# A log-sum-exp over rows of 1024: eighteen loads with another taper, a first load of two rows, and the second load ahead of the opening barrier

## The chip, the cores and the metric

The kernel runs on one core of one Trainium2 chip. The metric is the device time of one execution in microseconds (us), median of several. The *span* is shorter: it goes from the first to the last instruction of the program in the trace. Each timed run lists both. Two more words: the *opening barrier* is the point near the start of the program where the engines wait for each other, and the *taper* is the run of ever smaller loads at the end. Engines are named ScalarE (ACT), VectorE (DVE), GpSimd (POOL) and SyncE (SP); SyncE issues the loads.

## The reference

```python
x = np.random.randn(32, 512, 1024).astype(np.float32)      # 67 MB
x_max = np.max(x, axis=-1, keepdims=True)
out = x_max.squeeze(-1) + np.log(np.sum(np.exp(x - x_max), axis=-1))
```

16384 rows of 1024 are spread over 128 partitions, so each partition has 128 rows of 4 KB. The kernel leaves the maximum out, which the values allow, and computes log(sum(exp(x))).

## The kernel before

A list says how many rows each load takes, how many of them VectorE sums (ScalarE sums the rest with its accumulator), in how many pieces ScalarE takes VectorE's rows, and whether VectorE adds the two halves of each row in one pass:

```python
CHUNKS = [   # rows, rows summed by VectorE, pieces, by halves
    (4, 4, 1, False), (15, 15, 1, False), (16, 16, 2, False), (16, 16, 2, False),
    (16, 15, 2, False), (14, 14, 2, False), (13, 12, 2, False), (9, 8, 1, False),
    (7, 7, 1, True), (5, 4, 1, True), (4, 3, 1, True), (3, 3, 1, False), (2, 2, 1, True),
    (1, 0, 1, False), (1, 0, 1, False), (1, 0, 1, False), (1, 0, 1, False),
]
RING_ROWS = 51          # the loads land in a ring of 51 rows per partition
```

```python
    def load(i):        # waits until the engines have left these rows of the ring
        ...
        nc.sync.dma_start(out=ring[:, s : s + r], in_=x_v[:, row : row + r]).then_inc(landed[i], 16)
    ...
    load(0)
    n_early = len(body.instructions)        # what is there so far goes ahead of the opening barrier
    ...
    for i, (r, n_dve, parts, by_halves) in enumerate(CHUNKS):
        if i:
            load(i)
        ...
        if i == len(CHUNKS) - 1:            # logarithm of all but the last four rows
            take_logs(logged, late_row, sums[:, logged:late_row], *done_before[-LATE])
        nc.scalar.wait_ge(landed[i], 16)
        for lo, hi in cuts(n_dve, parts):
            nc.scalar.activation(out=ring[:, s+lo : s+hi], in_=ring[:, s+lo : s+hi], func=Exp).then_inc(act_done, 1)
            ...                             # VectorE sums these rows, row by row by halves or all at once
        for j in range(n_dve, r):
            nc.scalar.activation(..., func=Exp, accum_out=total(row + j)).then_inc(act_done, 1)
    take_logs(late_row, NB, late[:, : NB - late_row], dves, acts)
    nc.scalar.dma_start(out=out_v, in_=res).then_inc(stored, 16)
```

The sizes shrink so that the last load is a single row.

The softmax here doesn't subtract the row's maximum and nothing guards it: scores larger than these inputs give would overflow.

Of the kernel before, what the change touches and what calls it, by code (L numbers as in the profile page):

```python
# [8 lines left out]


CHUNKS = [
    (4, 4, 1, False), (15, 15, 1, False), (16, 16, 2, False), (16, 16, 2, False),
    (16, 15, 2, False), (14, 14, 2, False), (13, 12, 2, False), (9, 8, 1, False),
    (7, 7, 1, True), (5, 4, 1, True), (4, 3, 1, True), (3, 3, 1, False), (2, 2, 1, True),
    (1, 0, 1, False), (1, 0, 1, False), (1, 0, 1, False), (1, 0, 1, False),
]
RING_ROWS = 51

# [8 lines left out]
def kernel(  # L27
# [57 lines left out]
    def cuts(n, parts):  # L85
        ends = [-(-n * k // parts) for k in range(parts + 1)]
        return [(lo, hi) for lo, hi in zip(ends, ends[1:]) if lo < hi]

    def load(i):
        (s, row), r = place[i], CHUNKS[i][0]  # L90
        act_wait = max(a for a, _ in busy[s : s + r])
        dve_wait = max(d for _, d in busy[s : s + r])
        if dve_wait:
            nc.sync.wait_ge(dve_done, dve_wait)
        if act_wait:
            nc.sync.wait_ge(act_done, act_wait)
        nc.sync.dma_start(out=ring[:, s : s + r], in_=x_v[:, row : row + r]).then_inc(
            landed[i], 16
        )

    def take_logs(lo, hi, src, dve_wait, act_wait):
        nonlocal acts
        nc.scalar.wait_ge(act_done, act_wait)
        nc.scalar.wait_ge(dve_done, dve_wait)
        nc.scalar.activation(out=res[:, lo:hi], in_=src, func=Ln).then_inc(act_done, 1)  # L105
        acts += 1
# [4 lines left out]
    def total(t):  # L111
        return late[:, t - late_row : t - late_row + 1] if t >= late_row else sums[:, t : t + 1]

    body = nc.main_func.blocks[-1]
    assert not body.instructions
    load(0)
    n_early = len(body.instructions)

    nc.scalar.preload_act_table_set("natural_log_exp_and_others")  # L119
# [1 line left out]
    logged = 0  # L121
    done_before = [(0, 0)]
    for i, (r, n_dve, parts, by_halves) in enumerate(CHUNKS):
        if i:
            load(i)
        s, row = place[i]
        if i == LN_AT:
            logged = place[i - LN_LAG][1]
            take_logs(0, logged, sums[:, :logged], *done_before[i - LN_LAG])
        if i == len(CHUNKS) - 1:  # L130
# [3 lines that stand above are left out]
            nc.scalar.activation(  # L134
                out=ring[:, s + lo : s + hi], in_=ring[:, s + lo : s + hi], func=Exp
            ).then_inc(act_done, 1)
            acts += 1
            nc.vector.wait_ge(act_done, acts)
            if by_halves:
                for j in range(lo, hi):  # L140
                    nc.vector.tensor_tensor_reduce(  # L141
                        out=ring[:, s + j, : D // 2],
                        in0=ring[:, s + j, : D // 2],
                        in1=ring[:, s + j, D // 2 :],
                        scale=1.0,
                        scalar=0.0,
                        op0=Add,
                        op1=Add,
                        accum_out=sums[:, row + j : row + j + 1],
                    ).then_inc(dve_done, 1)  # L150
                    dves += 1
                    busy[s + j] = (0, dves)
            else:
                nc.vector.reduce_sum(  # L154
                    out=sums[:, row + lo : row + hi], in_=ring[:, s + lo : s + hi], axis=AX
                ).then_inc(dve_done, 1)
                dves += 1
                for j in range(lo, hi):
                    busy[s + j] = (0, dves)
        for j in range(n_dve, r):  # L160
            nc.scalar.activation(  # L161
                out=ring[:, s + j],
                in_=ring[:, s + j],
                func=Exp,
                accum_out=total(row + j),
            ).then_inc(act_done, 1)
            acts += 1
            busy[s + j] = (acts, 0)
        done_before.append((dves, acts))
# [64 lines left out]
```

## Time and profile before

| | before |
|---|---|
| time, median of 3 runs | 163.15 us |
| span of the profiled run | 161.4 us |
| input queue busy | 96.9% of the span |
| ScalarE, VectorE busy | 71%, 75% |
| last exponential starts | 158.46 us |

The lines that carry this stand in the prediction. One more belongs here, the end of VectorE's timeline (start, duration, instruction): the last step of its last sum, by halves of one row.

```profile
158.14 0.08 DVE L141 DVE_READ_ACCUMULATOR2_ANT sums<- 128x1 f32 x1
```

It ends at 158.22, and ScalarE's logarithm of these sums starts at 158.32. The last row is in at 158.4: its load was issued at 130.2 and took 28.2.

### The profile page before, as it was taken

To read this page: it belongs to the slowest core of one execution; us is meant where nothing else is said; L and a number is where in the kernel's file an instruction comes from. 1 tells how busy PE (TensorE), PEld (TensorE's weight loads), DVE (VectorE), ACT (ScalarE), POOL (GpSimd) and SP (SyncE) were. 2 spreads that over 40 slices of the span, in tenths; PEclk is the share of its full clock that TensorE was granted. 3 is DMA by queue.
4 is the path that set the end of the run, shared out by engine and by line. 5 is a ranking of instruction groups with operands and counts; after the bars stand their busy time and mean duration, and the time that the engine had idled before them with its cause. 6 is when DMAs were issued, how large, how long until landed. Compare 5 with 4: busy or idle time off the path is not lost.

```text
span 161.4 us, 149 instructions
## 1 busy us (share of the span) xinstructions
DVE 121.0 (75%) x46; ACT 115.1 (71%) x40; POOL 0.2 (0%) x4
## 2 busy tenths in 40 slices
DVE  0028000003999999999999699999999999999892
ACT  3170005996079960999519993999199999999995
POOL 0000000000000000000000000000000000000000
DMA  6999699989989989989979999999999999999990
GB/s 256 508 487 457 289 472 520 406 374 520 422 357 520 406 374 520 406 374 520 406 341 455 455 455 439 422 422 422 430 429 429 418 426 415 427 430 417 403 394 24
DMA packets 2592, 67.18 MB, mean 416 GB/s; under 512 B 288, under 2 KB 416, under 8 KB 928
## 3 DMA queue, kind: packets, MB, share of 16 engines
q1 hardware_dynamic: 2448, 67.11, 96.9%
q10 hardware_dynamic: 144, 0.07, 0.1%
HBM read 67.11 MB, written 0.07 MB: 416 GB/s over the span
## 4 chain that ended last, share of the span: by engine, by line
DMA 49%; DVE 29%; ACT 20%; issue 0%
DMA ring<-in_x_dram 49%; DVE sums L154 29%; ACT ring L134 17%; ACT ring L161 3%; ACT res L105 0%
## 5 line engine op out<-in xcount | busy, mean ns | idle before, releaser
L154 DVE TENSOR_REDUCE sums<-ring 128x8 f32<-128x8192 f32 (+5 forms) x14 | 111.2, 7995 | 37.3 <-ACT ring L134 37.2
L134 ACT ACTIVATE ring<-ring 128x8192 f32<-128x8192 f32 (+6 forms) x18 | 104.4, 5835 | 43.9 <-DMA ring<-in_x_dram 43.8
L141 DVE CUSTOM_DVE_ANT_0 ring<-ring 128x512 f32<-128x512 f32 x16 | 9.9, 688 | 0.0
L161 ACT ACTIVATE ring<-ring 128x1024 f32<-128x1024 f32 x9 | 9.3, 1041 | 0.0
L119 ACT ACT_TABLE_LOAD x1 | 1.3, 1283 | 0.8 <-PEq L215 0.8
L161 ACT ACTIVATION_READ_ACCUMULATOR ring<-ring 128x1 f32 x9 | 1.5, 172 | 0.0
L141 DVE DVE_READ_ACCUMULATOR2_ANT sums<- 128x1 f32 x16 | 1.3, 84 | 0.0
L105 ACT ACTIVATE res<-sums 128x81 f32<-128x81 f32 (+1 forms) x2 | 0.5, 246 | 0.0
L105 ACT ACTIVATE res<-late 128x4 f32<-128x4 f32 x1 | 0.2, 173 | 0.0
L215 POOL MEMSET const-bfloat16-1.0<- 128x1 bf16 x1 | 0.1, 103 | 0.0
L215 POOL MEMSET const-uint8-127<- 128x1 uint8 x1 | 0.1, 102 | 0.0
L215 POOL MEMSET const-float32-0.0<- 128x1 f32 x1 | 0.1, 100 | 0.2 <-issue 0.2
L215 POOL MEMSET const-float32-1.0<- 128x1 f32 x1 | 0.1, 99 | 0.0
## 6 DMA issues: line engine op xcount, KB each, us to landing
ring<-in_x_dram SPq DMA_DIRECT2D x1, 7680.0 KB, 25.2
ring<-in_x_dram SPq DMA_DIRECT2D x1, 7168.0 KB, 28.6
ring<-in_x_dram SPq DMA_DIRECT2D x1, 6656.0 KB, 35.7
ring<-in_x_dram SPq DMA_DIRECT2D x1, 4608.0 KB, 20.2
ring<-in_x_dram SPq DMA_DIRECT2D x2, 2048.0 KB, 16.1
ring<-in_x_dram SPq DMA_DIRECT2D x1, 3584.0 KB, 28.3
ring<-in_x_dram SPq DMA_DIRECT2D x1, 2560.0 KB, 27.3
ring<-in_x_dram SPq DMA_DIRECT2D x4, 512.0 KB, 27.0
```

What stands on the lines that cost most here:

```text
L105: nc.scalar.activation(out=res[:, lo:hi], in_=src, func=Ln).then_inc(act_done, 1)
L119: nc.scalar.preload_act_table_set("natural_log_exp_and_others")
L134: nc.scalar.activation(out=ring[:, s + lo : s + hi], in_=ring[:, s + lo : s + hi], func=Exp).then_inc(act_done, 1)
L141: nc.vector.tensor_tensor_reduce(out=ring[:, s + j, : D // 2], in0=ring[:, s + j, : D // 2], in1=ring[:, s + j, D // 2 :], scale=1.0, scal ...
L154: nc.vector.reduce_sum(out=sums[:, row + lo : row + hi], in_=ring[:, s + lo : s + hi], axis=AX).then_inc(dve_done, 1)
L161: nc.scalar.activation(out=ring[:, s + j], in_=ring[:, s + j], func=Exp, accum_out=total(row + j),).then_inc(act_done, 1)
L215: nc = _bacc.Bacc("TRN2", target_bir_lowering=False, num_devices=1)
```

## The change

The intent: data reach the engines earlier (two rows first, the second load issued before the barrier), and less work is left when the last row lands (a finer taper).

```diff
 CHUNKS = [
-    (4, 4, 1, False), (15, 15, 1, False), (16, 16, 2, False), (16, 16, 2, False),
-    (16, 15, 2, False), (14, 14, 2, False), (13, 12, 2, False), (9, 8, 1, False),
-    (7, 7, 1, True), (5, 4, 1, True), (4, 3, 1, True), (3, 3, 1, False), (2, 2, 1, True),
-    (1, 0, 1, False), (1, 0, 1, False), (1, 0, 1, False), (1, 0, 1, False),
+    (2, 2, 1, False), (14, 14, 1, False), (14, 14, 1, False), (13, 13, 2, False),
+    (15, 15, 2, False), (14, 13, 2, False), (13, 13, 2, False), (12, 9, 2, False),
+    (7, 7, 2, False), (7, 7, 1, True), (5, 4, 1, False), (3, 3, 2, True), (3, 3, 1, True),
+    (2, 2, 1, True), (1, 0, 1, False), (1, 0, 1, False), (1, 0, 1, False), (1, 0, 1, False),
 ]
@@
     load(0)
+    load(1)
     n_early = len(body.instructions)
@@
-        if i:
+        if i > 1:
             load(i)
```

## The prediction

In its lines of ScalarE's timeline, brackets hold the idle time before an instruction and what ended it. In its table of half microseconds the columns are the stretch, its length, the busy time (and count) of VectorE, ScalarE and GpSimd, TensorE's clock (not used here), the DMA engines' share and GB/s.

The 433 GB/s is what the queue moved. The sum comes to 0.07 us of queue and 0.06 of rounding and ScalarE lateness, 0.13 together, and 163.15 + 0.13 - 0.1 gives the centre of 163.2. The 0.1 for the start is my estimate of how much of the measured 0.67 and 0.34 could be cured. The 0.15 of start in VectorE's 14 x 1.067 + 0.15 follows from the rows by form: 3 rows take 3.353, and 3.353 - 3 x 1.067 = 0.15. The "nearer 1 us" to the first byte is this kernel's: issue at 0.00, nothing moved before 1.00.

> **What bounds the kernel now.** I read the page first: what is busy, then which chain ended last. All 128 rows of 4 KB per partition come in through one queue, and that queue is busy nearly all the time.
>
> ```profile
> span 161.4 us, 149 instructions
> DVE 121.0 (75%) x46; ACT 115.1 (71%) x40; POOL 0.2 (0%) x4
> ...
> q1 hardware_dynamic: 2448, 67.11, 96.9%
> ```
>
> The reader should see that VectorE and ScalarE have a quarter of the span to spare, while the input queue fills 96.9% of it. So the middle is a matter of bytes, and only the two ends can be shortened. ScalarE's timeline gives the landings of the large loads, because in the middle it waits for each:
>
> ```profile
> 7.49 3.62 ACT L134 ACTIVATE ring<-ring 128x4096 f32<-128x4096 f32 x1 [5.43 <-DMA ring<-in_x_dram]
> 25.99 13.00 ACT L134 ACTIVATE ring<-ring 128x15360 f32<-128x15360 f32 x1 [14.89 <-DMA ring<-in_x_dram]
> 45.36 13.95 ACT L134 ACTIVATE ring<-ring 128x8192 f32<-128x8192 f32 x2 [6.36 <-DMA ring<-in_x_dram]
> ...
> 84.08 13.10 ACT L134 ACTIVATE ring<-ring 128x8192 f32<-128x8192 f32 x2 [5.39 <-DMA ring<-in_x_dram]
> ...
> 116.74 10.54 ACT L134 ACTIVATE ring<-ring 128x6144 f32<-128x6144 f32 x2 [3.49 <-DMA ring<-in_x_dram]
> ```
>
> From 45.36 to 84.08 two loads of 16 rows land: 19.36 us each. Last I read the end of the chain of waits:
>
> ```profile
> 122.44 24.70 DMA ring<-in_x_dram
> 147.14 0.02 issue
> 147.16 2.76 ACT ring L134
> 149.92 1.04 ACT ring L161 x2
> 150.96 4.45 ACT ring L134 x2
> 155.42 3.01 ACT ring L161 x6
> 158.43 0.01 ACT res L105
> 158.43 0.03 issue
> 158.46 1.11 ACT ring L161 x2
> ```
>
> From 116.74 (row 94) to 147.16 (row 119) 25 rows come in four loads, 30.42 us. At the big loads' rate, 25/16 x 19.36 = 30.25; the 0.17 too much is the price of 4 - 25/16 = 2.44 loads more, so one load costs 0.07 us and one row (19.36 - 0.07)/16 = 1.206 us. After 147.16 ScalarE waits for nothing and ends the kernel. It is hardly later than the data: the first load landed at 7.49, so its queue began, in effect, at 7.49 - 4 x 1.206 - 0.07 = 2.60; the second took 18.50 instead of 15 x 1.206 + 0.07 = 18.16, another 0.34; the last row is then due at 2.94 + 128 x 1.206 + 17 x 0.07 = 158.50, and ScalarE's last exponential began at 158.46. The model misses by 0.04 at most. So **transfer and ScalarE end together**. From 158.46 to the end (161.41) is 2.95 us of exponential, logarithm and store, which the change leaves alone.
>
> [...] 16 rows are 8.39 MB, in 19.36 us 433 GB/s. [...] Here the first issue is at 0.00 and the trace by half microseconds shows nothing before 1.00, so nearer 1 us, then a ramp:
>
> ```profile
> 0.50:1.00 0.50, 0.00 (x0) 0.23 (x1) 0.00 (x0) 1.00 0.00 0
> 1.00:1.50 0.50, 0.00 (x0) 0.50 (x1) 0.00 (x0) 1.00 1.11 229
> 1.50:2.00 0.50, 0.00 (x0) 0.50 (x1) 0.00 (x0) 1.00 0.68 197
> 2.00:2.50 0.50, 0.00 (x0) 0.06 (x1) 0.00 (x0) 1.00 0.69 295
> 2.50:4.50 2.00, 0.00 (x0) 0.00 (x0) 0.00 (x0) 1.00 1.03 442
> ```
>
> [...]
>
> **The change part by part.** ScalarE's price, from the rows by form: 13.002 us for 15 rows and 1.893 for 2 give 0.854 us a row and 0.18 an instruction. Back to back half of the 0.18 overlaps (two of 7.02 take 13.95), so an instruction costs 0.09 on the path. A row summed on ScalarE costs 1.04, in the last four loads 1.00 (they start at 155.32, 156.32, 157.32). VectorE: (16.154 - 3.353)/12 = 1.067 a row.
>
> *One load more.* 17 become 18 over the same 128 rows: +0.07 us of queue. The last row is due at 158.57.
>
> *Second load ahead of the barrier.* Its issue moves from 0.78 us to some 0.4. But it queues behind the first, which holds the queue until 7.49 now and until 2.60 + 2 x 1.206 + 0.07 = 5.1 with two rows. An issue at 0.78, with 1 us to its first byte, was there in time and still would be. Worth 0. The barrier and the table load behind it (1.28 us, from 0.77) come about 0.4 us later and end near 2.5, before the 5.1 at which ScalarE has data: 0.
>
> *First load of two rows.* ScalarE and VectorE begin 2.4 us earlier on two rows, then wait for the second load (16 rows, due 22.4). They have slack there: 0 for the end.
>
> *Middle sizes and the ring of 51 rows.* The first four loads now fill 43 rows and the fifth (15) wraps to slot 0, so it waits for VectorE on the second load: due 22.4, exponential 14 x 0.854 + 0.18 = 12.1, sum 14 x 1.067 + 0.15 = 15.1, so 49.7. The queue has work until 55.1. Before, it was issued at 55.21 and took 28.85 to land, of which 19.36 was its own: 9.5 us of slack, now 5.4. The next two have about 6.6 and 9.5, later ones more. It shrinks but stays above the 1 us that an idle queue takes to begin: 0.
>
> *The taper.* Due times (2.94 + 1.206 per row + 0.07 per load) of loads 8 to 18: 120.5, 129.0, 137.5, 143.6, 147.3, 151.0, 153.5, 154.7, 156.0, 157.3, 158.6. ScalarE on them, from 120.5:
> load 8 (9 rows in two, 3 summed) 9 x 0.854 + 0.18 + 3.12 = 11.0, to 131.5;
> load 9 (7 in two) 6.16, to 137.6;
> load 10 (7) 6.07, to 143.7;
> load 11 (4, 1 summed) 4.55, to 148.25;
> load 12 (3 in two) 2.74, to 151.0;
> load 13 (3) 2.65, to 153.65;
> load 14 (2) 1.80, to 155.45;
> three single rows 3.00, to 158.45; a logarithm 0.14, to 158.59; the last row then starts, its data due at 158.57.
> The two end together again, **0.13 later** than 158.46. What the taper does relieve is VectorE: its last sum ended at 158.2, just ahead of the logarithm at 158.32; by the same sums it should now end near 157.4. It was not holding anything.
>
> Sum: 0.07 of queue, with 0.06 of rounding and ScalarE lateness, so about +0.1 on 163.15.
>
> **The rivals.**
> *The start gains.* Between 1.0 and 2.5 us the queue moved 361 KB (721 x 0.5), where 433 GB/s would be 650: 0.67 us is lost there, partly while later loads are issued (0.78 to 2.4). If smaller first packets or the earlier issue cure all of it, and the 0.34 of the second load as well, the time is 162.2. [...] I give it 0.1 us on average.
> *The queue starves at the wrap.* Were VectorE 5 us later than reckoned on the second load, each us beyond would be added whole. For it: slack almost halves. Against: both durations come from rows of the same form. A miss of 1 us makes 164.2.
> *ScalarE becomes the bound in the taper.* Each late load adds directly, since ScalarE has no idle from 120.5 to the end by my sum. If each of its 21 or so instructions there cost 0.02 more, 0.4 us: 163.6.
> *The taper wins.* It cannot by much: even a ScalarE that is never late starts the last row when it lands, where it already starts now.
>
> **Range and chances.** Centre: 163.15 + 0.13 from the sum, less 0.1 for the start: 163.2 us. The three runs spread 0.36, and each rival moves some tenths: 162.7 to 163.8. Two per cent is 3.26 us; to gain it would need more than the whole ramp, to lose it a starved queue. Faster 0.015, within 2% 0.975, slower 0.01.
>
> **What would show it.** Right: the queue's share again near 97%; ScalarE's first exponential at about 5.1; the fifth load issued near 49.7 and still some 23 to 24 us from landing; ScalarE without idle from about 120.5; last exponential at 158.5 to 158.7; VectorE done near 157.4. Wrong: a dip of the rate where the fifth or sixth load begins (starved), an idle gap on ScalarE in the last 30 us (landings later than reckoned), or a first exponential clearly before 5.0 with everything after shifted by the same (the start gained).

## The result, and the profile after

The changed kernel took 163.43 us (median of 6 runs, 163.14 to 163.79), the kernel before beside it 163.19 (6 runs, 162.96 to 163.37). The ratio is 1.0014, with a 95% interval of 0.9998 to 1.003. The time is the same by any useful threshold; if anything it is 0.2 us longer.

The profile of the changed kernel (busy times with their shares of the span, then the input queue with packets, MB and share) has a span that is *shorter*:

```profile
span 161.0 us, 153 instructions
DVE 121.5 (75%) x46; ACT 115.3 (72%) x43; POOL 0.2 (0%) x4
...
q1 hardware_dynamic: 2592, 67.11, 97.3%
```

ScalarE's timeline at the start (start, duration, instruction, idle time before it and what ended it):

```profile
1.25 1.28 ACT L120 ACT_TABLE_LOAD   x1 [1.25 <-PEq L216]
4.99 1.91 ACT L135 ACTIVATE ring<-ring 128x2048 f32<-128x2048 f32 x1 [2.46 <-DMA ring<-in_x_dram]
21.93 12.15 ACT L135 ACTIVATE ring<-ring 128x14336 f32<-128x14336 f32 x1 [15.03 <-DMA ring<-in_x_dram]
```

The table load came half a microsecond later (1.25 for 0.77) and was over at 2.53, long before the first data at 4.99, as predicted. But the second load's 16 rows are in at 21.93, where the sum said 22.4.

The end of the chain of waits (start, duration, what), from the landing of load 8, the last for which ScalarE waited:

```profile
96.28 23.67 DMA ring<-in_x_dram
119.95 0.02 issue
119.97 7.97 ACT ring L135 x2
127.95 3.12 ACT ring L162 x6
131.06 15.73 ACT ring L135 x4
146.80 1.04 ACT ring L162 x2
147.84 7.20 ACT ring L135 x4
155.04 1.93 ACT ring L162 x3
156.97 0.92 issue
157.89 0.17 ACT ring L162
158.05 0.03 ACT res L105
158.09 1.11 ACT ring L162 x2
```

From 119.97 on ScalarE does not wait (the "issue" of 0.92 is the third single row's exponential, which the chain doesn't count as such). The prediction had this stretch from 120.5 to 158.6; here it is from 119.97 to 158.07, so the whole list lies half a microsecond earlier and is as long as worked out: 38.1 us in both. VectorE is done a microsecond before that:

```profile
156.84 0.08 DVE L142 DVE_READ_ACCUMULATOR2_ANT sums<- 128x1 f32 x1
```

The span of the profiled run is 0.4 us shorter and its time 163.15 us, which is 2.1 us more than its span. Before, time minus span was 163.28 - 161.4 = 1.9. The six runs of the changed kernel all have 2.08 to 2.15.

### The profile page after: what moved, and what is told of

The parts are those of the page before. It is cut to its first block, busy times and chain, and to the rows that moved or that the text cites. A ratio compares the mean times of both kernels' runs of the same rounds, so it can differ in the third digit from the quotient of the medians. Undisturbed runs are those within 1.5% of the kernel's fastest.

```text
span 161.0 us, 153 instructions
## 1 busy us (share of the span) xinstructions
DVE 121.5 (75%) x46; ACT 115.3 (72%) x43; POOL 0.2 (0%) x4
## 4 chain that ended last, share of the span: by engine, by line
DMA 38%; ACT 31%; DVE 28%; issue 1%
DMA ring<-in_x_dram 38%; DVE sums L155 28%; ACT ring L135 27%; ACT ring L162 5%; ACT res L105 0%
## 5 line engine op out<-in xcount | busy, mean ns | idle before, releaser
L155 DVE TENSOR_REDUCE sums<-ring 128x7 f32<-128x7168 f32 (+7 forms) x16 | 112.3, 7079 | 35.1 <-ACT ring L135 35.1
L135 ACT ACTIVATE ring<-ring 128x7168 f32<-128x7168 f32 (+8 forms) x21 | 104.6, 5028 | 42.8 <-DMA ring<-in_x_dram 42.8
L142 DVE CUSTOM_DVE_ANT_0 ring<-ring 128x512 f32<-128x512 f32 x15 | 9.3, 687 | 0.3 <-ACT ring L135 0.3
L105 ACT ACTIVATE res<-sums 128x72 f32<-128x72 f32 (+1 forms) x2 | 0.5, 248 | 0.0
```

Of the source, the lines that this page charges most:

```text
L105: nc.scalar.activation(out=res[:, lo:hi], in_=src, func=Ln).then_inc(act_done, 1)
L135: nc.scalar.activation(out=ring[:, s + lo : s + hi], in_=ring[:, s + lo : s + hi], func=Exp).then_inc(act_done, 1)
L142: nc.vector.tensor_tensor_reduce(out=ring[:, s + j, : D // 2], in0=ring[:, s + j, : D // 2], in1=ring[:, s + j, D // 2 :], scale=1.0, scal ...
L155: nc.vector.reduce_sum(out=sums[:, row + lo : row + hi], in_=ring[:, s + lo : s + hi], axis=AX).then_inc(dve_done, 1)
```

## The experiments

Three questions: what the start is worth, what the taper is worth, and where the time outside the span comes from. My theory going in was the prediction's: the start is worth nothing, the end is a balance of transfer, ScalarE and VectorE that can be added up. The rival for the start was a gain of some tenths that something else gives back. Twelve experiments ran, the last of them the changed kernel again; eleven have six timed runs and one has four. The first four ran on one chip, the other eight on another. Times below are medians of these runs; spans, and time minus span, are means over them; single points of time are from each kernel's profile.

### The start

**The kernel before with the second load early.**

```diff
     load(0)
+    load(1)
     n_early = len(body.instructions)
```

(The loop then issues its loads from the third on.)

> The kernel before with only its second load moved ahead of the opening barrier; loads and taper as before. My theory (the second load queues behind the first, so its issue time is worth nothing): within 0.1 us of the kernel before, second landing still about 18.2 to 18.5 us after the first, ScalarE table load about 0.4 us later. Rival 'the start gains': 0.3 to 0.5 us faster, because the issue of the second load no longer falls into the ramp of the first (1.0 to 2.5 us), and the second load lands 0.3 us sooner after the first. Rival 'the barrier costs': about 0.2 us slower although the landings are the same, since the barrier comes later.

Measured: 163.17 us, ratio 0.9996 (0.9984 to 1.0009), time minus span 1.87. The second load's exponential started at 25.73; in the runs that have four and fifteen rows first and the second load late, it starts anywhere from 25.49 to 26.12. The table load came at 1.24 us for 0.77. So neither rival holds: moving this issue gains or costs nothing that these runs can tell, which is some 0.2 us.

**The changed kernel with the second load late again.**

```diff
     load(0)
-    load(1)
     n_early = len(body.instructions)
```

> The changed kernel with its second load behind the barrier again. My theory: same as the changed kernel within 0.1 us, so ratio to the kernel before 1.0005 to 1.0015; even with a first load of two rows the queue is not empty before the second load's first bytes (issue at 0.78, bytes from about 1.8, first load done near 4.6). Rival 'the start gains': 0.3 to 0.5 us slower than the changed kernel. Rival 'the barrier costs': 0.2 us faster than the changed kernel, ratio about 1.000.

Measured: 163.51 us, ratio 1.001 (0.9996 to 1.0023); span 161.33, as the changed kernel's 161.28. Its time minus span was 2.10, so the early issue is not the cause of the time outside the span either. Even with only two rows ahead of it the second load is in time: ScalarE's exponential of the first load starts at 4.80, that of the second here.

```profile
21.72 12.15 ACT L134 ACTIVATE ring<-ring 128x14336 f32<-128x14336 f32 x1 [15.01 <-DMA ring<-in_x_dram]
```

**A first load of two rows with the taper of the kernel before.**

```diff
-    (4, 4, 1, False), (15, 15, 1, False), (16, 16, 2, False), (16, 16, 2, False),
-    (16, 15, 2, False), (14, 14, 2, False), (13, 12, 2, False), (9, 8, 1, False), ...
+    (2, 2, 1, False), (16, 16, 1, False), (16, 16, 2, False), (16, 16, 2, False),
+    (16, 15, 2, False), (15, 15, 2, False), (13, 12, 2, False), (9, 8, 1, False), ...
```

(The second load is early here too.)

> A first load of two rows with the taper of the kernel before: 2, 16, 16, 16, 16, 15, 13, then 9, 7, 5, 4, 3, 2 and four of 1 as before, 17 loads, second load early. The sums of the prediction carried on for VectorE: it has summed only two rows when the second load's 16 are ready near 38.6, so it ends its last sum about 0.7 us later, near 158.9 instead of 158.2, and the logarithm before the last row waits for it: 0.5 to 0.7 us slower than the kernel before (ratio 1.003 to 1.004). Rival 'the start gains': faster by 0.2 to 0.5, as data arrive earlier. Rival 'VectorE does not matter': within 0.1.

Measured: 163.50 us, ratio 1.0014 (1.0 to 1.0027), span 161.60 beside 161.44. The expected loss of 0.5 to 0.7 us did not come, only about a third of it (0.23 by the ratio). The mechanism is there, in the logarithm ahead of the last row:

```profile
158.33 0.24 ACT L102 ACTIVATE res<-sums 128x43 f32<-128x43 f32 x1 [0.51 <-DVE sums L139]
```

ScalarE sat idle 0.51 us for VectorE, whose last sum ended at 158.23. By the sums it should have been 158.9: everything lay some 0.6 earlier, because the transfer did. The start does gain, and the prediction's zero for it is wrong. Over all profiles: with two rows first (seven with 14 rows next) the second load's exponential starts at 21.62 to 21.93, mean 21.73; with four and fifteen (six profiles) at 25.49 to 26.12, mean 25.74. Three rows at 1.206 are 3.62, so at equal rows the two-row start is 25.74 - 3.62 - 21.73 = **0.39 us ahead**. Of this 0.22 is there at the first landing (4.65 to 4.99, mean 4.80, beside 7.37 to 7.49, mean 7.43, less 2 x 1.206 = 2.41). This run, which has 16 rows next, agrees: its second landing is at 24.18, which at equal rows is 25.74 - 1.206 - 24.18 = 0.35 ahead. Why the smaller first load starts better these runs do not show.

### The taper

**The kernel before up to row 94, then the changed kernel's taper.**

```diff
     (16, 15, 2, False), (14, 14, 2, False), (13, 12, 2, False),
-    (9, 8, 1, False), (7, 7, 1, True), (5, 4, 1, True), (4, 3, 1, True), (3, 3, 1, False), (2, 2, 1, True), ...
+    (3, 2, 1, False), (7, 7, 2, False), (7, 7, 1, True), (5, 4, 1, False), (3, 3, 2, True), (3, 3, 1, True), (2, 2, 1, True), ...
```

> The head of the kernel before up to row 94, then a load of 3 rows and the changed kernel's last ten loads (7, 7, 5, 3, 3, 2 and four of 1), 18 loads, second load late. By the sums: one load more (0.07), VectorE ends near 158.7 and the logarithm waits 0.3 for it, last exponential at about 158.8: 0.3 to 0.4 us slower than the kernel before (ratio 1.002). Rival 'the finer taper helps by itself': equal or faster. Rival 'one more load is the whole cost': 0.07 slower.

Measured: 163.58 us, ratio 1.0018 (1.0004 to 1.0031), span 161.72 beside 161.44: 0.28 longer. The logarithm waited 0.19 us for VectorE, and VectorE ended at 158.71, against 158.7 by the sums:

```profile
158.81 0.24 ACT L102 ACTIVATE res<-sums 128x43 f32<-128x43 f32 x1 [0.19 <-DVE sums L138]
158.63 0.08 DVE L138 DVE_READ_ACCUMULATOR2_ANT sums<- 128x1 f32 x1
```

The finer taper by itself does not help; it loses about what the sums say, a little less than the 0.3 to 0.4 expected.

**The changed kernel with the two splits in its taper undone.**

```diff
-    (7, 7, 2, False), (7, 7, 1, True), (5, 4, 1, False), (3, 3, 2, True), ...
+    (7, 7, 1, False), (7, 7, 1, True), (5, 4, 1, False), (3, 3, 1, True), ...
```

> The changed kernel with the two splits in its taper taken back: the first load of 7 rows and the first load of 3 rows in one exponential each, so two ScalarE and two VectorE instructions fewer. Two questions. Inside the span: ScalarE saves 2 x 0.09, but VectorE gets the same rows later; by the sums its last sum ends near 158.8 instead of 157.4 and the logarithm before the last row waits 0.4 for it: span 0.3 to 0.4 longer than the changed kernel's (mean 161.3, so 161.6 to 161.7). Outside the span: in the runs so far time minus span is 1.87 to 1.89 for the kernel before and for three of the variants, but 2.12 for the changed kernel and 2.10 for the changed kernel with the late second load. If that comes with the number of ScalarE instructions (51, 51, 51, 52 against 54, 54 in the traces), this one with 52 has 1.88; if with the list of loads, 2.1.

Measured: 163.58 us, span 161.65, 0.37 longer than the changed kernel's 161.28 as reckoned, and time minus span 1.86. The two splits buy VectorE an earlier start, and without them the logarithm waits:

```profile
158.06 0.25 ACT L102 ACTIVATE res<-sums 128x52 f32<-128x52 f32 x1 [0.34 <-DVE sums L139]
```

So the two splits are worth 0.37 us inside the span, and the kernel with them has 0.26 us more outside of it (2.12 less 1.86).

**The changed kernel with the last four rows in one load.**

```diff
-    (1, 0, 1, False), (1, 0, 1, False), (1, 0, 1, False), (1, 0, 1, False),
+    (4, 0, 1, False),
-LATE = 4
+LATE = 1
```

> The changed kernel with its last four rows in one load instead of four (15 loads). The queue saves 3 x 0.07 and ends near 158.3, but after that landing ScalarE has four rows to do instead of one: last exponential starts 3 x 1.0 later. Theory 'the taper was already as fine as pays': this one is 2.7 to 3.0 us slower than the changed kernel (ratio to the kernel before 1.016 to 1.019), which shows the size of what a taper can give and that both kernels already have it. Rival 'the taper is worth little': below 1 us.

Measured (four runs): 166.14 us, ratio 1.018 (1.0158 to 1.0203), so slower than the kernel before, though whether by two per cent is unclear; span 164.05, 2.77 longer than the changed kernel's. ScalarE waited for the load until 158.00 and had four rows to go, one a microsecond:

```profile
158.00 1.06 ACT L159 ACTIVATE ring<-ring 128x1024 f32<-128x1024 f32 x1 [0.68 <-DMA ring<-in_x_dram]
```

The fourth starts at 161.01. This is what the last four single-row loads are worth, and both kernels already have them.

**The transfer alone.** The changed kernel with every exponential and sum on 16 of 1024 elements; its result is wrong.

```diff
-    out=ring[:, s + lo : s + hi], in_=ring[:, s + lo : s + hi], func=Exp
+    out=ring[:, s + lo : s + hi, :16], in_=ring[:, s + lo : s + hi, :16], func=Exp
```

(The sums are cut likewise. The 0.25 us expected for the last exponential is an estimate; in the changed kernel ScalarE's logarithm of 52 elements took 0.25.)

> The changed kernel, all loads and waits as they are, but each exponential and sum on 16 of the 1024 elements of a row: a wrong result on purpose, to measure the transfer alone. My theory (the transfer and ScalarE end together): the last row lands where it landed in the changed kernel, about 158.0 to 158.5, and the time is shorter only by the last exponential, which takes some 0.25 instead of 1.06: 0.7 to 0.9 us faster than the changed kernel, ratio to the kernel before about 0.996. Rival 'ScalarE or VectorE holds the kernel, the transfer has room': over 1.5 us faster. Rival 'the loads wait for the ring': the last landing comes clearly sooner, since here every load is issued early.

Measured: 162.58 us, ratio 0.9961 (0.9943 to 0.9978); span 160.48, 0.80 shorter than the changed kernel's. ScalarE now waits for each single row, and the last is in at 158.3. In the changed kernel it landed at 158.0, in that kernel's second profile (below) at 158.3, so no sooner here:

```profile
158.34 0.21 ACT L163 ACTIVATE ring<-ring 128x16 f32<-128x16 f32 x1 [0.83 <-DMA ring<-in_x_dram]
```

All of the engines' work is hidden behind the transfer but for the last row's exponential. And since the loads here are issued early and still land no sooner, the ring of 51 rows does not hold the changed kernel back, though its slack shrank as predicted (the fifth load was issued at 49.23, of which the prediction said 49.7).

### What lies outside the span

The page counts 40 ScalarE instructions before and 43 after; with the eleven of its sequencer the trace has 51 and 54. The expectations use these larger counts.

**The kernel before with three ScalarE instructions more.**

```diff
+        if i == 0:
+            for k in range(3):
+                nc.scalar.activation(out=scratch[:, k:k+1], in_=nc.const_aps.tensor(0.0, (P, 1), fp32), func=Exp)
```

> The kernel before with three ScalarE instructions more (one element of a constant each, to a scratch tile, ahead of the first exponential, where ScalarE has 15 us to spare before the second load). Theory 'more ScalarE instructions lengthen what lies outside the span': span as before (161.4), time minus span 2.1 instead of 1.87, so about 0.23 us slower in time. Rival 'it is something else in the list of loads': time minus span stays 1.87 and the time is as before within 0.1.

Measured: 163.24 us; span 161.18 beside 161.28; time minus span 2.06 to 2.15, mean **2.12**, where the kernel before has 1.84 to 1.92. Its ratio, 1.0005 (0.9987 to 1.0024), can't tell a fifth of a microsecond; time minus span can, as the two ranges do not touch.

**The kernel before with four GpSimd instructions more.**

```diff
+    for k in range(4):
+        nc.gpsimd.memset(scratch[:, k : k + 1], 0.0)
```

> The kernel before with four GpSimd fills of one element more, which nothing waits for. If time minus span grows with the instructions of the whole program (149 before, 153 in the changed kernel), it is 2.1 here; if with ScalarE's alone, or with neither, 1.87.

Measured: time minus span 1.89, so it is not the number of instructions in the whole program. The time was 162.95, ratio 0.9985 (0.9967 to 1.0003), for a kernel that does the same work with the same loads: a ratio of this size, the main result's included, shows nothing by itself.

**The kernel before with nineteen ScalarE instructions more** (the same lines with 19 for 3).

> The kernel before with nineteen ScalarE instructions more (one constant element each, ahead of the first exponential, 4 us of the 15 that ScalarE has to spare there). 70 ScalarE instructions in the trace. If what lies outside the span grows with the count in proportion (0.23 for three), time minus span is 3 us or more; if it is one step between 52 and 54, 2.1; if there is a step for every some fifteen instructions, 2.3 to 2.4. Span as before, 161.3 to 161.4.

Measured: 163.92 us, ratio 1.0049 (1.0025 to 1.0073). All three guesses failed. Time minus span is back at 1.87, but the span is 162.15, 0.89 longer. The exponentials kept their places (the last at 158.53); the store's issue took 1.18 us where it takes 0.37 in the kernel before (next two fences: the store in this kernel, "ACTq" being ScalarE's sequencer, and in the kernel before with durations in ns):

```profile
159.87 1.18 ACTq L177 DMA_DIRECT2D out_dram<-res  x1
```

```profile
L173 ACTq DMA_DIRECT2D out_dram<-res x1: 373/373/373, 159.8 to 159.8; - x1
```

And the list of queues on its page has a line that the page of the kernel before doesn't have:

```profile
q14 instruction: 1, 0.01, 0.0%
```

One packet of this queue, whose kind the page gives as "instruction", moved inside the span, at about 159.5 by the trace, and the store's issue took 0.81 us longer. That the packet held up the store fits the order of events but is not shown; it is read from one profile.

**A list meant to beat both.**

```diff
+    (2, 2, 1, False), (14, 14, 1, False), (16, 16, 2, False), (15, 15, 2, False),
+    (10, 10, 1, False), (13, 13, 2, False), (12, 12, 2, False), (11, 11, 2, False),
+    (10, 10, 2, False), (7, 7, 1, True), (5, 5, 1, True), (4, 4, 1, True), (3, 3, 1, True),
+    (2, 2, 1, False), (1, 0, 1, False), (1, 0, 1, False), (1, 0, 1, False), (1, 0, 1, False),
```

> A list of loads meant to beat both: 18 loads, two rows first, second load early, but only four rows summed on ScalarE instead of nine and 20 exponentials instead of 21, so 43 ScalarE instructions in the trace (54 in the changed kernel), VectorE sums more of the taper by halves (60 instructions instead of 52). By the sums the last exponential starts when the last row lands (158.5), so the span is 0.1 shorter than the changed kernel's, 161.2. Time minus span: 1.87 if the 0.23 us come with ScalarE's instructions beyond 52 alone; about 2.1 if VectorE's count does the same; below 1.87 if there is another step between 43 and 51. Time 163.0 to 163.1, ratio to the kernel before 0.999 in the first case.

Measured: 163.38 us, ratio 1.001 (0.9991 to 1.003). The span, 161.22, is as reckoned, the shortest of the correct versions with a two-row start by 0.06, which is within the scatter; time minus span is 2.05 to 2.29, mean 2.17, with 43 ScalarE instructions and 60 of VectorE. So "beyond 52 of ScalarE" is not the rule. It beats nothing. Its trace has one packet of kind "instruction" 1.9 us after the end of the span; the trace of the changed kernel has none in its span or after it.

**The changed kernel again, beside the kernel before.**

> The changed kernel once more, beside the kernel before on the same chip. Span 161.2 to 161.4 and time minus span 2.10 to 2.12, so a ratio of 1.000 to 1.002 with all of the loss outside the span.

Measured: 163.45 us, ratio 1.0012 (0.9993 to 1.0032). Span 161.28 beside 161.26, time minus span 2.14 beside 1.88: no difference inside the span, all of it outside. (Of the kernel before, 11 of the 12 runs are those that the batch of experiments before it lists too.)

| kernel | ScalarE / VectorE instructions | mean span | time minus span |
|---|---|---|---|
| before, on the first chip (11 runs); on the second (12) | 51 / 52 | 161.44; 161.26 | 1.87; 1.88 |
| before, second load early | 51 / 52 | 161.33 | 1.87 |
| changed; again | 54 / 52 | 161.28; 161.28 | 2.12; 2.14 |
| changed, second load late | 54 / 52 | 161.33 | 2.10 |
| changed, last four rows in one load | 54 / 52 | 164.05 | 2.10 |
| changed, transfer alone | 54 / 52 | 160.48 | 2.09 |
| changed, splits undone | 52 / 51 | 161.65 | 1.86 |
| before with the changed taper | 52 / 52 | 161.72 | 1.88 |
| before, two rows first | 51 / 52 | 161.60 | 1.89 |
| before + 4 GpSimd | 51 / 52 | 161.08 | 1.89 |
| before + 3 ScalarE | 54 / 52 | 161.18 | 2.12 |
| before + 19 ScalarE | 70 / 52 | 162.15 | 1.87 |
| fewer ScalarE | 43 / 60 | 161.22 | 2.17 |

The number of loads does not decide it either: 15 loads (last four rows in one) have 2.10, 18 (before with the changed taper) have 1.88.

## Why the prediction was right or wrong

The time was inside the range, the same within 2%. The centre, 163.2, is 0.23 below the measured median of 163.43. Two things that the sum held at nothing, or nearly so, did move: the start gained, and the time outside the span grew. They pull in opposite directions, so that the number came so close is in part luck.

*"Second load ahead of the barrier ... Worth 0."* Right within some 0.2 us: shown from both sides, without it and with it alone.

*"First load of two rows ... 0 for the end."* This term failed. ScalarE's slack there was argued rightly, but the transfer itself starts better: 0.39 us at the second landing. The rival "the start gains" had the right sign, and the 0.1 that I allowed for it was too little. The prediction's own sign for it, a first exponential clearly before 5.0 and everything after shifted, came: 4.99 in the first profile, 4.65 to 4.89 in the seven others that start with two rows. At the end less is left of it. The last row lands at 158.27 in the mean of the five profiles with the loads of the kernel before (issue plus time to landing; 157.91 to 158.57), and at 158.12 in that of the five with the changed kernel's loads (157.70 to 158.32), where the sum had it 0.07 later: some 0.2 of the 0.39. (The prediction's model, 158.50 for the kernel before, was thus 0.23 late in the mean and 0.12 in its own profile, not the 0.04 that it says, because it took ScalarE's start for the landing.) The last exponential began at 158.07 in the profile where the sum said 158.59, but single profiles scatter. The mean span is between 0.16 us shorter (beside the first batch of the kernel before) and 0.02 longer (beside the second), where the sum had it 0.13 longer; so by the spans, too, 0.1 to 0.3 us arrives.

*"One load more. ... +0.07 us of queue"* and *"The taper ... 0.13 later".* ScalarE's 38.1 us from load 8's landing to the last exponential were right, VectorE ended at 156.9 for 157.4, half a microsecond early like everything else in that profile. The experiments that change only this part move the span by 0.28 (sum: 0.3 to 0.4), 0.37 (0.3 to 0.4) and 2.77 (2.7 to 3.0). The taper's sums hold to a tenth of a microsecond. The price of one load, 0.07, is not tested by itself: it comes from one profile, and landings scatter by more.

*"It shrinks but stays above the 1 us ... 0."* Right, by the transfer alone.

*"From 158.46 to the end (161.41) is 2.95 us ... which the change leaves alone."* Right inside the span (158.07 to 161.04 is 2.97). What I did not write is that I took the time to be the span plus a constant. **That step failed**: the constant went from 1.87 to 2.12, and that is the whole of the measured difference. Three idle ScalarE instructions added to the kernel before reproduce the 0.25, so the loads and the taper are not needed for it. It is not a matter of more instructions: with nineteen it is gone, and there a packet of kind "instruction" (at about 159.5) comes just ahead of a store whose issue takes 0.81 us longer inside the span. That such a packet near the end is the cause of both is my guess and not shown. For the nineteen the trace has the packet. Of the kernels with more time outside the span, the list with fewer ScalarE instructions has one 1.9 us after its span, but the changed kernel has none in its span or after it. Why the five kernels with 54 instructions of ScalarE, and the one with 43 and 60 of VectorE, have the 0.25, and those with 51, 52 and 70 don't, stays open.

The intent itself fell short because nothing was left at the end to gain: the last exponential before already began within 0.1 us of the last row's landing, and the transfer fills 97% of the span.

## What to carry to other kernels

Add up transfer, first engine and second engine to the last landing before touching a taper. Here the queue was busy for 97% of the span and the three met within a quarter of a microsecond; the finer taper by itself made the span 0.28 us longer, with ScalarE waiting 0.19 us for VectorE. Ask what else is in the queue, and not only when a load is issued: here the second load was issued long before the first landed at 7.4 us, behind the barrier or ahead of it, and moving its issue gave a ratio of 0.9996. For differences of a few tenths of a microsecond compare time and span apart, and add a few instructions that do nothing as a control: three of them moved the time outside the span here by 0.25 us, as much as the change did, and nineteen lengthened the span by 0.89.

## What else the traces show

- Nothing moved in the first 1.0 us from the start of the first issue, before and after. The issue itself takes 0.37 us, so from its end it is 0.63.
- The eighteenth load's issue takes long. In the changed kernel and in the one with the transfer alone it took 3.7 and 22.4 us and came to its end near 132 in both, though begun at 128.1 and 109.7. With seventeen loads the longest issue is 0.8 us. What it waits for is not shown. It cost nothing here, since nothing follows it on that engine. SyncE's issues with the transfer alone (count, then minimum, median and maximum in ns, first and last start in us):

```profile
L98 SPq DMA_DIRECT2D ring<-in_x_dram x18: 327/428/22437, 0.0 to 109.7; - x18
```
